# Order of DVE and ACT at seven places of a decoder layer, and products with v ahead of the scores

## The chip, the cores and the metric

The kernel runs on one core of one Trainium2 chip. The metric is device time in microseconds (us). A core has engines that run their own instruction queues in order and meet through semaphores: TensorE (PE, matrix products), VectorE (DVE), ScalarE (ACT), GpSimd (POOL) and SyncE (SP, which here issues transfers). Matrix products accumulate in PSUM; everything else lives in SBUF.

## The reference

One decoder layer on x of 1024 positions by 1024 features, in float32, with a pre-norm on each sub-layer. The mixer has two branches that are merged by gates; a gated MLP with a causal convolution of width 3 follows.

```
h = rmsnorm(x)
q, k, v, su, sv, g_a, g_b = split(h @ w_in)
y_att = sliding_window_attention(q, k, v)      # window 128, 8 query and 2 key heads of 64, ALiBi, sinks
y_sgu = gelu(su) * (tril(w_s) @ rmsnorm(gelu(sv)) + b_s)   # in chunks of 128 positions, 8 groups
x = x + (sigmoid(g_a) * (y_att @ w_oa) + sigmoid(g_b) * (y_sgu @ w_ob)) @ w_out
z = conv(rmsnorm(x) @ w_up)                    # per channel, over positions
gate, val = split(z)
x = x + (silu(gate) * val) @ w_down
```

The hidden width of the MLP is 2816, so w_up has 5632 columns (22 pairs of a gate block and a value block).

## The kernel before

**Precision.** Every float32 operand of a large product is split in a high part, rounded to PE's float32r by ACT (`copy_hi`, line 88), and a low part, the difference, taken by DVE or POOL. A product is three matmuls: high by high, high by low, low by high (`mm3`, lines 92 to 94). Lines 1120, 1700 and 2055 do the same in the later stages. So each operand passes ACT, then DVE or POOL, before PE reads it.

**Blocks.** From the gates on, products are done on two by two blocks with seven block products and sums of blocks (A11, B11, S1 to S4 and T1 to T4 are such blocks and sums). Sums are added on DVE while their parts sit in PSUM.

**Stages.** The span runs through: x, k and v, and the first q (to 45 us); the attention loop (`for n in range(20)`, to about 170); the spatial gating unit (`v_phase`, `v_end`, to 220); the gates; the branches (`B_UNITS`, y as the right operand, 355 to 445); the output product (`out_job`, 14 of them, 445 to 530); the MLP's up product with 22 pairs (`fast_pair`, to 960); the down product in seven products M1 to M7 (`mms`, to the end).

**What sets the order.** Every engine runs its instructions in the order in which the code issues them: the whole body is under a manual schedule. So the order of the lines is the order of the queues, and an instruction that waits holds all behind it on its engine.

**What the change touches.**

- k's evacuation: `k_hi` and `k_lo` empty a transposed k from PSUM (tile pk) into the high and low parts kT, one instruction for each of two row halves (line 397). `q_sq`, `q_ms`, `q_norm` square q's projection (tile pq), take its mean and the power on POOL (line 324, tile qss), and normalize it (line 330, tile qr). `v_evac` (line 407) scales v by rstd, a power on POOL (line 447), and line 140 spreads rstd over the partitions by matmuls (tile rb). `q_split` ends in the low parts qs (line 345).
- The attention loop is software-pipelined: step n issues scores of block n (`s_mm`, lines 484 and 487, tile sc), mask and maximum, exponentials of n-1, transposes and splits of n-2 (`p_trans`, `p_split`), products with v of n-4 (`pv_mm`, line 559, tile pv) and their result (`pv_out`, line 572, tile ya). A filler of projections stands between.
- The gating unit: `sgu_seed` (ACT, line 979) writes the bias into a PSUM tile pm, `sgu_mm` adds a product, `sgu_mul` (DVE, line 996, tile uT) multiplies the result into u and so empties the tile. `v_rsqrt`, `v_norm` and `v_split` prepare v for it.
- The branches: `y_split(br, n, eng)` makes the high (line 88) and low part (line 1294) of a block y; `hooks` are called between the products of a unit. Line 1360 is the low part of the weights (wjl, on POOL).
- The output: after product j = 0 and 1, ACT copies the result X to Y (line 1708), into which later products add. `O_WORK[j]` issues splits for coming products.
- `fast_pair`: the sums of a pair need x1, an ACT copy of one block product (line 1888). `prev.tap_v()` is the first tap of the convolution of the pair before (ACT, line 1741), `prev.last_sum()` the DVE sum and scale that it reads.
- The down product: `mms(g)` runs a group of k tiles, for each k over four rows d of output; `done(s)` adds a finished product to the result on DVE (`plus`, line 2092). The accumulators X are two PSUM tiles pdx with two rows d each.

Of the kernel before, what the change touches and what calls it, by code (L numbers as in the profile page):

```python
# [14 lines left out]
ALU = mybir.AluOpType  # L15
# [25 lines left out]
def body(ctx, tc, nc, a):  # L41
# [349 lines left out]

    def k_lo(h):
        cs = slice(512 * h, 512 * h + 512)
        pk = st.pop(("pk", h))
        for g in range(2):
            r = ROWS[g]
            nc.vector.scalar_tensor_tensor(kTl[r, g, cs], pk[r, :], kgq[r, 0:1], kTh[r, g, cs].bitcast(F),
                                           op0=ALU.mult, op1=ALU.subtract)
# [39 lines left out]
    q_proj(2)  # L438
    k_lo(0)
    q_norm(1)  # L440
    k_twice(0)
    q_trans(0)
# [3 lines left out]
    k_norm(1)  # L446
    nc.gpsimd.tensor_tensor(rstd, rstd, mh05, op=ALU.pow)
    q_split(0)
    q_norm(2)
    copy_hi(u_next[0], u_raw[0])  # L450
    nc.gpsimd.tensor_tensor(u_next[1], u_raw[0], u_next[0].bitcast(F), op=ALU.subtract)
    v_evac(0)
    v_evac(1)
    q_trans(1)
    k_trans(1)
    q_sq(3)
    q_split(1)
    q_ms(3)
    nc.vector.tensor_scalar(nsink, sink_b, -1.0, None, op0=ALU.mult)
    k_hi(1)  # L460
    rms_rows([PH("rb")], rstd, (0,))
    k_lo(1)
# [225 lines left out]
    man.__enter__()  # L688
    for n in range(20):
        if n < 16:  # L690
            s_mm(n)
            s_mask(n)
# [4 lines left out]
        if n < 16:  # L697
            s_max(n)
        if 0 <= n - 4 < 16:
            pv_mm(n - 4)  # L700
# [141 lines left out]
    def v_phase():  # L842
# [8 lines left out]
        for s in range(7):  # L851
            v_half(s, 1)
            if 4 <= s + 3 < 8:
                v_half(s + 3, 0)
            if s == 6:
                sgu_mm(0, 0)
            v_gelu(s)
            wb_copy(s)
            if s < 4:
                nc.scalar.activation(uT[:, s, :], uT[:, s, :], AF.Gelu_apprx_tanh)  # L860
            v_rsqrt(s)
            if s < 5:
                v_norm(s)
            if s in X_WORK:
                X_WORK[s]()
            if s > 0:
                v_split(s - 1)
            if s == 6:
                sgu_mul(0, 0)
            if s > 4:  # L870
                v_norm(s)
            if s in X_LATE:
                X_LATE[s]()
# [431 lines left out]
    def gates():  # L1305
# [6 lines left out]
        un["hooks"][1, 0] = lambda: (y_split("a", "T4"), y_split("a", "T1", nc.gpsimd))  # L1312
        un["hooks"][2, "x"] = lambda: (y_split("a", "T2", nc.gpsimd), y_hi("a", "B22"))
        un["hooks"][2, 0] = lambda: y_lo("a", "B22")
# [374 lines left out]
    def out_job(j):  # L1689
# [3 lines left out]
        def main(w):  # L1693
# [3 lines left out]
            for d in (0, 1):  # L1697
                for k in range(4):
                    for i, (p, q) in enumerate(((w[0], 0), (w[0], 1), (w[1], 0))):
                        nc.tensor.matmul(ob[o][e][:, d, :], p[:, 4 * d + k, :], m[:, q, k, :],  # L1700
                                         start=s in (0, 5) and k == 0 and i == 0, stop=k == 3 and i == 2,
                                         skip_group_check=True)
            O_WORK.get(j, lambda: None)()
            yield
            if j == 0:
                ob["Y"] = [PS("pY").rearrange("p (d c) -> p d c", d=2) for _ in range(2)]
            if s == 0:
                nc.scalar.copy(ob["Y"][e], ob["X"][e])
            else:
                {10: post10, 11: post11, 12: post12, 13: post13}.get(j, lambda: o_post(s, e))()  # L1710
# [159 lines left out]
    def fast_pair(n, prev, q, hooks, rms=None):  # L1870
# [6 lines left out]
        if rms:  # L1877
            x1 = temp("x1f", "wx")
        else:
            prev.last_sum()  # L1880
            prev.tap_v()
            x1, x7, q.u2 = temp("x1"), temp("x7"), temp("u2")
# [3 lines left out]
        if not nx:  # L1886
            hooks[2]()
        nc.scalar.copy(x1, q.g0)  # L1888
        if rms:
            rms()  # L1890
# [57 lines left out]
    def mlp():  # L1948
# [93 lines left out]
        def mms(g):  # L2042
# [8 lines left out]
            for k in range(k0, k1):  # L2051
                for d in range(4):
                    m = slice(128 * d, 128 * d + 128)
                    for j, (p, q) in enumerate(((ah, bh), (ah, bl), (al, bh))):
                        nc.tensor.matmul(o[d], p[:, k - k0, m], q[:, k - k0, :],  # L2055
                                         start=new and k == 0 and j == 0, stop=k == HK - 1 and j == 2,
                                         skip_group_check=True)

        def mms_last():

# [80 lines left out]
        for g in range(len(groups)):  # L2141
            if g < len(groups) - 2:
                mms(g)
# [111 lines left out]
```

## Time and profile before

| | us |
|---|---|
| median of 3 runs | 1163.71 (1163.32 to 1163.99) |
| profiled execution | 1162.16, span 1160.1 |
| PE busy | 1152.5 (99%), 5784 matmuls |
| DVE, ACT, POOL busy | 853.1 (74%), 589.9 (51%), 662.5 (57%) |
| DMA | 204.37 MB, 176 GB/s in the mean; granted clock of PE 0.999 |

Busy times are of the one profiled execution. In the rows of a timeline the first two numbers are the start from the span's beginning and the duration in us; then engine, line of the kernel, operation, output<-inputs by the program's names, sizes, and how many like instructions are merged (their duration is from the first start to the last end). The bracket is the idle time of the engine just before and what ended it. Matmuls overlap, so the distance of starts, not the duration, is what one costs. PE idles before its first matmul and after its last (the last results are written out from about 1156.4 on); between these the idle time is a few waits, each under 0.6 us.

### The profile page before, as it was taken

What the parts mean: (1) busy time and instruction counts of PE and PEld (TensorE: products, weight loads), DVE (VectorE), ACT (ScalarE), POOL (GpSimd) and SP (SyncE); (2) the same over time, 40 slices, a digit from 0 to 9 for tenths busy, and PEclk for the clock granted to TensorE, in tenths of its full rate; (3) what the DMA queues carried; (4) which work ended last, traced back from release to release, by engine and by line L of the source; (5) the groups of instructions that cost most, each with busy time, mean ns of one, the idle gap of its engine ahead of it and who ended that gap; (6) DMA issues with size and microseconds to landing.
All of it is one profiled execution on the core that took longest, in us unless ns stands there. A gap on an engine that the chain in (4) does not pass through costs nothing.

```text
span 1160.1 us, 15819 instructions
## 1 busy us (share of the span) xinstructions
PE 1152.5 (99%) x5784; PEld 978.5 (84%) x5784; DVE 853.1 (74%) x985; ACT 589.9 (51%) x896; POOL 662.5 (57%) x462
## 2 busy tenths in 40 slices
PE   9999999999999999999999999999999999999998
PEld 9999999888888888888888888888888888888887
DVE  7777746734537889877888878797878887766674
ACT  6665568643436546676544444444444454425231
POOL 1668684597883844798877676767676730000000
PEclk9999999999999999999999999999999999999999
DMA  9442575266646766634655554545464368965571
GB/s 365 150 146 57 133 220 191 92 187 194 191 118 227 244 218 236 190 128 129 163 173 138 162 129 143 160 140 139 134 171 132 97 216 301 356 219 199 175 228 55
DMA packets 86429, 204.37 MB, mean 176 GB/s; under 512 B 9616, under 2 KB 17296, under 8 KB 86160
## 3 DMA queue, kind: packets, MB, share of 16 engines
q1 hardware_dynamic: 77280, 174.93, 43.7%
q0 software_dynamic: 8544, 19.93, 10.5%
q10 hardware_dynamic: 528, 8.52, 2.1%
q8 instruction: 45, 0.74, 0.3%
q14 instruction: 32, 0.26, 0.1%
HBM read 162.70 MB, written 57.41 MB: 190 GB/s over the span
## 4 chain that ended last, share of the span: by engine, by line
PE 85%; DVE 5%; POOL 3%; DMA 2%; ACT 2%; issue 1%; SPq 0%; DVEq 0%; ACTq 0%; POOLq 0%
PE pz L1120 51%; PE pdx L2055 10%; PE pd L2055 8%; PE pY L1700 2%; PE pX L1700 1%; PE pu L94 1%; PE pu L92 1%; PE pu L93 1%; PE pv L559 1%; DMA xr<-xw 1%; PE pq L92 1%; PE pq L94 1%; PE pq L93 1%; POOL sq L1547 1%; DMA xt<-xt 1%
## 5 line engine op out<-in xcount | busy, mean ns | idle before, releaser
L1120 PE MATMUL pz<-T,qh 128*128 128x512 f32 x464 | 143.0, 389 | 0.0
L1120 PE MATMUL pz<-B,ph 128*128 128x512 f32 x352 | 108.9, 390 | 0.5 <-ACT x L1888 0.4
L1120 PEld LDWEIGHTS pz<-T,qh 128*128 128x128 f32 x464 | 87.0, 188 | 18.4 <-ACT u L937 0.3
L1072 POOL TENSOR_TENSOR pl<-lp,ph 128x1024 fp32r<-128x1024 f32 x30 | 73.7, 2456 | 36.3 <-ACT ph L88 36.3
L1120 PE MATMUL pz<-T,ql 128*128 128x512 f32 x232 | 90.2, 389 | 0.0
L1138 DVE TENSOR_TENSOR pz<-pz,rstd_b 128x1024 f32<-128x1024 f32 x60 | 74.0, 1232 | 6.1 <-ACT rstd_b L143 4.1
L1120 PEld LDWEIGHTS pz<-B,ph 128*128 128x128 f32 x352 | 65.8, 188 | 14.7 <-ACT x L1888 1.3
L1072 POOL TENSOR_TENSOR ql<-lq,qh 128x1024 fp32r<-128x1024 f32 (+1 forms) x31 | 76.5, 2490 | 0.1
L1120 PE MATMUL pz<-T,s3h 128*128 128x512 f32 x232 | 71.4, 389 | 0.0
L1120 PE MATMUL pz<-y,wjh 128*128 128x512 f32 x224 | 69.6, 391 | 0.4 <-POOL y L1294 0.4
L1120 PE MATMUL pz<-B,pl 128*128 128x512 f32 x176 | 68.5, 389 | 0.0
L88 ACT ACTIVATE qh<-lq 128x1024 fp32r<-128x1024 f32 (+1 forms) x31 | 31.5, 1021 | 67.7 <-POOL pl L1072 50.3
L1072 POOL TENSOR_TENSOR s3l<-lq,s3h 128x512 fp32r<-128x512 f32 x20 | 26.0, 1300 | 68.2 <-ACT s3h L88 68.2
L2055 PE MATMUL pdx<-bh,ah 128*128 128x512 f32 x164 | 63.9, 390 | 0.1
L2055 PE MATMUL pdx<-bl,ah 128*128 128x512 f32 x164 | 63.8, 389 | 0.0
L2055 PE MATMUL pdx<-bh,al 128*128 128x512 f32 x164 | 63.8, 389 | 0.0
L1360 POOL TENSOR_TENSOR wjl<-wj,wjh 128x512 fp32r<-128x512 f32 (+1 forms) x32 | 41.9, 1329 | 33.7 <-ACT wjh L88 27.0
L1120 PE MATMUL pz<-T,AX 128*128 128x512 f32 x252 | 60.5, 389 | 0.0
L1120 PE MATMUL pz<-B,AX 128*128 128x512 f32 x252 | 60.5, 389 | 0.0
L1746 DVE SCALAR_TENSOR_TENSOR tg<-pz,cp,tg 128x1023 f32<-128x1023 f32 (+1 forms) x44 | 56.2, 1278 | 0.8
L1746 DVE SCALAR_TENSOR_TENSOR tv<-pz,cp,tv 128x1023 f32<-128x1023 f32 (+1 forms) x44 | 56.2, 1278 | 0.8
L1120 PEld LDWEIGHTS pz<-T,AX 128*128 128x128 f32 x252 | 47.3, 188 | 9.8
(392 smaller groups left out, 3574.7 us busy)
## 6 DMA issues: line engine op xcount, KB each, us to landing
lp<-wup SPq DMA_DIRECT2D x22, 512.0 KB, 3.8
lq<-wup SPq DMA_DIRECT2D x22, 512.0 KB, 4.0
ra<-wdown SPq DMA_DIRECT2D x44, 256.0 KB, 4.6
b<-T SPq DMA_DIRECT2D x44, 256.0 KB, 3.4
lq<-wup POOLq DMA_DIRECT2D x42, 256.0 KB, 5.4
B<-tv SPq DMA_DIRECT2D x33, 256.0 KB, 2.4
T<-tt SPq DMA_DIRECT2D x33, 256.0 KB, 2.2
b<-B SPq DMA_DIRECT2D x33, 256.0 KB, 3.0
```

The costliest lines, as they stand in the source:

```text
L88: return nc.scalar.activation(dst, src, AF.Copy, scale=scale)
L92: nc.tensor.matmul(out, wh, mh, start=first, stop=False, **kw)
L93: nc.tensor.matmul(out, wh, ml, start=False, stop=False, **kw)
L94: nc.tensor.matmul(out, wl, mh, start=False, stop=last, **kw)
L559: nc.tensor.matmul(o, vhl[:, kb, g, :], w[:, 2 * g:2 * g + 2, :], start=i == 0 and g == 0, stop=i == len(ops) - 1, skip_group_check=True)
L1072: nc.gpsimd.tensor_tensor(l, r, h.bitcast(F), op=ALU.subtract)
L1120: nc.tensor.matmul(o, p[:, k, :], m, start=not more and k == 0 and j == 0, stop=k == nk - 1 and j == 2, skip_group_check=True)
L1138: nc.vector.tensor_tensor(z, z, rstd_b, op=ALU.mult)
L1360: nc.gpsimd.tensor_tensor(l[:, k], r[:, k], h[:, k].bitcast(F), op=ALU.subtract)
L1700: nc.tensor.matmul(ob[o][e][:, d, :], p[:, 4 * d + k, :], m[:, q, k, :], start=s in (0, 5) and k == 0 and i == 0, stop=k == 3 and i == 2, ...
L1746: nc.vector.scalar_tensor_tensor(t[:, j:], p[:, 0:1024 - j], cw[:, ci, 2 - j:3 - j], t[:, j:], op0=ALU.mult, op1=ALU.add)
L2055: nc.tensor.matmul(o[d], p[:, k - k0, m], q[:, k - k0, :], start=new and k == 0 and j == 0, stop=k == HK - 1 and j == 2, skip_group_check= ...
```

## The change

The places, numbered in the order of the program, as the prediction names them:

1. k's evacuation: the two low parts of the first half of k are split, with `q_norm(1)` between them. The power of rstd goes ahead of that of q 2 on POOL. `v_evac(0)` goes ahead of `q_norm(2)`, `v_evac(1)` behind `q_split(1)`, and on ACT the copy of the spread rstd ahead of `k_hi(1)`.
2. Attention: in the steps 4 to 11 the products with v are issued ahead of the scores (on PE alone).
3. Gating unit: `sgu_mul(0, 0)` goes ahead of `v_rsqrt(6)` and `v_split(5)`.
4. Branches: the low part of y block T2 of branch a is taken by DVE instead of POOL.
5. Output: the copy after product 1 is issued ahead of that product's `O_WORK`.
6. and 7. Up product: in pairs 2 and 3 the copy x1 goes ahead of `prev.tap_v`.
8. Down product: the last two groups of M5 are run together, all k of a row d before the next d (`mms_two`).

```diff
--- before.py
+++ after.py
@@ -389,10 +389,10 @@
         for g in range(2):
             copy_hi(kTh[ROWS[g], g, cs], pk[ROWS[g], :], scale=kgq[ROWS[g], 0:1])
 
-    def k_lo(h):
+    def k_lo(h, gs=(0, 1)):
         cs = slice(512 * h, 512 * h + 512)
-        pk = st.pop(("pk", h))
-        for g in range(2):
+        pk = st[("pk", h)]
+        for g in gs:
             r = ROWS[g]
             nc.vector.scalar_tensor_tensor(kTl[r, g, cs], pk[r, :], kgq[r, 0:1], kTh[r, g, cs].bitcast(F),
                                            op0=ALU.mult, op1=ALU.subtract)
@@ -436,29 +436,30 @@
     k_trans(0)
     k_hi(0)
     q_proj(2)
-    k_lo(0)
+    k_lo(0, (0,))
     q_norm(1)
+    k_lo(0, (1,))
+    nc.gpsimd.tensor_tensor(rstd, rstd, mh05, op=ALU.pow)
     k_twice(0)
     q_trans(0)
     q_proj(3)
     q_sq(2)
     q_ms(2)
     k_norm(1)
-    nc.gpsimd.tensor_tensor(rstd, rstd, mh05, op=ALU.pow)
     q_split(0)
-    q_norm(2)
     copy_hi(u_next[0], u_raw[0])
     nc.gpsimd.tensor_tensor(u_next[1], u_raw[0], u_next[0].bitcast(F), op=ALU.subtract)
     v_evac(0)
-    v_evac(1)
+    q_norm(2)
     q_trans(1)
     k_trans(1)
     q_sq(3)
     q_split(1)
+    v_evac(1)
     q_ms(3)
     nc.vector.tensor_scalar(nsink, sink_b, -1.0, None, op0=ALU.mult)
+    rms_rows([PH("rb")], rstd, (0,))
     k_hi(1)
-    rms_rows([PH("rb")], rstd, (0,))
     k_lo(1)
     v_split()
     k_twice(1)
@@ -687,6 +688,8 @@
     man = tc.manual_schedule()
     man.__enter__()
     for n in range(20):
+        if 4 <= n < 12:
+            pv_mm(n - 4)
         if n < 16:
             s_mm(n)
             s_mask(n)
@@ -696,7 +699,7 @@
             s_exp(n - 1)
         if n < 16:
             s_max(n)
-        if 0 <= n - 4 < 16:
+        if 12 <= n:
             pv_mm(n - 4)
         q_new = filler(n, 0)
         if 0 <= n - 2 < 16:
@@ -858,6 +861,8 @@
             wb_copy(s)
             if s < 4:
                 nc.scalar.activation(uT[:, s, :], uT[:, s, :], AF.Gelu_apprx_tanh)
+            if s == 6:
+                sgu_mul(0, 0)
             v_rsqrt(s)
             if s < 5:
                 v_norm(s)
@@ -865,8 +870,6 @@
                 X_WORK[s]()
             if s > 0:
                 v_split(s - 1)
-            if s == 6:
-                sgu_mul(0, 0)
             if s > 4:
                 v_norm(s)
             if s in X_LATE:
@@ -1310,7 +1313,7 @@
         un["hooks"][0, 0] = lambda: y_split("a", "B21", nc.gpsimd)
         un["hooks"][1, "x"] = lambda: y_split("a", "T3")
         un["hooks"][1, 0] = lambda: (y_split("a", "T4"), y_split("a", "T1", nc.gpsimd))
-        un["hooks"][2, "x"] = lambda: (y_split("a", "T2", nc.gpsimd), y_hi("a", "B22"))
+        un["hooks"][2, "x"] = lambda: (y_split("a", "T2"), y_hi("a", "B22"))
         un["hooks"][2, 0] = lambda: y_lo("a", "B22")
         nc.vector.tensor_scalar(ng2, g2, -1.0, None, op0=ALU.mult)
         un["hooks"][3, 1] = lambda: (m_split("B11", 0), m_sum("T1", 0))
@@ -1700,13 +1703,15 @@
                         nc.tensor.matmul(ob[o][e][:, d, :], p[:, 4 * d + k, :], m[:, q, k, :],
                                          start=s in (0, 5) and k == 0 and i == 0, stop=k == 3 and i == 2,
                                          skip_group_check=True)
+            if j == 1:
+                nc.scalar.copy(ob["Y"][1], ob["X"][1])
             O_WORK.get(j, lambda: None)()
             yield
             if j == 0:
                 ob["Y"] = [PS("pY").rearrange("p (d c) -> p d c", d=2) for _ in range(2)]
-            if s == 0:
-                nc.scalar.copy(ob["Y"][e], ob["X"][e])
-            else:
+            if j == 0:
+                nc.scalar.copy(ob["Y"][0], ob["X"][0])
+            elif j > 1:
                 {10: post10, 11: post11, 12: post12, 13: post13}.get(j, lambda: o_post(s, e))()
             O_AFTER.get(j, lambda: None)()
             if j == 13:
@@ -1878,7 +1883,8 @@
             x1 = temp("x1f", "wx")
         else:
             prev.last_sum()
-            prev.tap_v()
+            if n not in (2, 3):
+                prev.tap_v()
             x1, x7, q.u2 = temp("x1"), temp("x7"), temp("u2")
         q.prod(q.g0, "A11", "B11")
         if rms:
@@ -1886,6 +1892,8 @@
         if not nx:
             hooks[2]()
         nc.scalar.copy(x1, q.g0)
+        if n in (2, 3):
+            prev.tap_v()
         if rms:
             rms()
             lefts[n].split_r(n)
@@ -2056,6 +2064,16 @@
                                          start=new and k == 0 and j == 0, stop=k == HK - 1 and j == 2,
                                          skip_group_check=True)
 
+        def mms_two(g):
+
+            two = [(k, k - groups[i][1], ops_[i]) for i in (g - 1, g) for k in range(*groups[i][1:])]
+            for d in range(4):
+                m = slice(128 * d, 128 * d + 128)
+                for k, i, (ah, al, bh, bl) in two:
+                    for j, (p, q) in enumerate(((ah, bh), (ah, bl), (al, bh))):
+                        nc.tensor.matmul(X[d], p[:, i, m], q[:, i, :], start=False,
+                                         stop=k == HK - 1 and j == 2, skip_group_check=True)
+
         def mms_last():
 
             two = [(k, k - groups[g][1], ops_[g]) for g in (len(groups) - 2, len(groups) - 1)
@@ -2139,7 +2157,9 @@
         q = prev
         n_load = 4
         for g in range(len(groups)):
-            if g < len(groups) - 2:
+            if g == 6 * len(GR) - 1:
+                mms_two(g)
+            elif g < len(groups) - 2 and g != 6 * len(GR) - 2:
                 mms(g)
             s, k0, k1 = groups[g]
             while n_load < min(g + 6, len(groups)):
```

What DVE does at k's evacuation, before (pq and qr are of q, pk and kT of k, vt of v):

```order
L397 SCALAR_TENSOR_TENSOR kT_107<-pk_515,kgq,kT_107 64x512 x2
L330 TENSOR_TENSOR qr_549<-pq_477,qss_507 128x256
L322 TENSOR_REDUCE qss_583<-qsq_581 128x4
L323 TENSOR_SCALAR qss_583<-qss_583,eps_x 128x4
L376 TENSOR_TENSOR kr<-pkv_126,krs 128x512
L345 TENSOR_TENSOR qs_589<-pqt_553,qs_589 64x256 x2
L330 TENSOR_TENSOR qr_594<-pq_522,qss_583 128x256
L407 TENSOR_TENSOR vt<-pkv_125,rstd 128x512
L407 TENSOR_TENSOR vt<-pkv_126,rstd 128x512
L345 TENSOR_TENSOR qs_610<-pqt_600,qs_610 64x256 x2
```

and now:

```order
L397 SCALAR_TENSOR_TENSOR kT_107<-pk_515,kgq,kT_107 64x512
L330 TENSOR_TENSOR qr_548<-pq_477,qss_507 128x256
L397 SCALAR_TENSOR_TENSOR kT_107<-pk_515,kgq,kT_107 64x512
L322 TENSOR_REDUCE qss_584<-qsq_582 128x4
L323 TENSOR_SCALAR qss_584<-qss_584,eps_x 128x4
L376 TENSOR_TENSOR kr<-pkv_126,krs 128x512
L345 TENSOR_TENSOR qs_589<-pqt_554,qs_589 64x256 x2
L407 TENSOR_TENSOR vt<-pkv_125,rstd 128x512
L330 TENSOR_TENSOR qr_597<-pq_522,qss_584 128x256
L345 TENSOR_TENSOR qs_609<-pqt_599,qs_609 64x256 x2
L407 TENSOR_TENSOR vt<-pkv_126,rstd 128x512
```

`q_norm(1)` (qr_548) now stands between the two kT, the first vt ahead of the next qr, and the low parts of the next q ahead of the second vt.

What ACT does at the start of pair 2, before (tv and tg are taps of the pair before, x_731 is x1, pz are PSUM tiles):

```order
L1132 COPY u_716_5646<-pz_5443 128x512
L88 ACTIVATE AX_5638<-lr_5710 128x1024
L1741 ACTIVATE tv_5768<-pz_5443,cp 128x1024
L1888 COPY x_731_5770<-pz_5764 128x512
L1741 ACTIVATE tg_5786<-pz_5442,cp 128x1024
```

and now:

```order
L1135 COPY u_716_5646<-pz_5443 128x512
L88 ACTIVATE AX_5638<-lr_5710 128x1024
L1894 COPY x_730_5768<-pz_5764 128x512
L1746 ACTIVATE tv_5784<-pz_5443,cp 128x1024
L1746 ACTIVATE tg_5786<-pz_5442,cp 128x1024
```

The copy x1 (line 1894 now) and the tap tv have changed places; in pair 3 the same.

What DVE does in the branch unit with the y block T2 (y_539) and the block after it (y_503), before:

```order
L1400 TENSOR_TENSOR pz_4145<-u_534_4149,pz_4145 128x512
L1407 SCALAR_TENSOR_TENSOR m_4233<-th_4104,pz_4145 128x1024
L1407 SCALAR_TENSOR_TENSOR m_4235<-th_4106,pz_4146 128x1024
L663 TENSOR_TENSOR x_550_4240<-x_550_4240,pz_4237 128x512
L1294 TENSOR_TENSOR y_503_3990<-ya_3157,y_503_3990 128x1024
L1394 TENSOR_TENSOR pz_4238<-x_549_4239,pz_4238 128x512
```

and now:

```order
L1403 TENSOR_TENSOR pz_4145<-u_534_4149,pz_4145 128x512
L1410 SCALAR_TENSOR_TENSOR m_4233<-th_4104,pz_4145 128x1024
L1410 SCALAR_TENSOR_TENSOR m_4235<-th_4106,pz_4146 128x1024
L1297 TENSOR_TENSOR y_539_4191<-ta,y_539_4191 128x1024
L664 TENSOR_TENSOR x_550_4240<-x_550_4240,pz_4237 128x512
L1297 TENSOR_TENSOR y_503_3990<-ya_3157,y_503_3990 128x1024
L1397 TENSOR_TENSOR pz_4238<-x_549_4239,pz_4238 128x512
```

The low part y_539 has come in from POOL, between the products m of the unit before and the subtraction x; on POOL the weights' low parts (wjl) follow one another there.

## The prediction

> **What bounds the kernel now.** I read the busy shares first, then what PE waited for, then the timelines of the engines around each wait. PE is busy for 1152.5 of the 1160.1 us, and the change neither adds nor removes a matmul; all it can win is PE's idle time. The waits of PE, by cause (engine, tile and line that waited <- releaser: total us, times, longest):
>
> ```profile
> PE pq L92 <- DVE kT L397: 0.6, 1, 0.6
> PE pm L92 <- ACT pm L979: 0.5, 1, 0.5
> PE pz L1120 <- ACT x L1888: 0.4, 1, 0.4
> PE pz L1120 <- POOL y L1294: 0.4, 1, 0.4
> PE pY L1700 <- ACT pY L1708: 0.3, 1, 0.3
> ```
>
> Each happens once, and each lies at one of the places that the diff touches; a sixth, 0.20 us, is in the row at 43.25 below. Elsewhere PE issues without a break, so the sum goes place by place. A wait costs a little more than its idle time. Two pairs of rows (start us, duration us) show it:
>
> ```profile
> 566.94 0.39 PE L1120 MATMUL pz<-B,pl 128*128 128x512 f32 x1
> 569.66 0.39 PE L1120 MATMUL pz<-T,s3l 128*128 128x512 f32 x1
> 570.48 0.50 PE L1120 MATMUL pz<-B,ph 128*128 128x512 f32 x1 [0.43 <-ACT x L1888]
> 589.43 0.39 PE L1120 MATMUL pz<-T,s3l 128*128 128x512 f32 x1
> 589.85 0.73 PE L1120 MATMUL pz<-B,ph 128*128 128x512 f32 x2
> 568.75 1.21 ACT L1741 ACTIVATE tv<-pz,cp 128x1024 f32<-128x1024 f32 x1 [1.74 <-DVE pz L1138]
> 569.86 0.57 ACT L1888 COPY x<-pz 128x512 f32<-128x512 f32 x1
> ```
>
> Unhindered, such a matmul starts 0.23 us after the one before: two take 0.62 and one 0.39 in the rows at 396.44 and 569.66. From 569.66 to 570.48 are 0.82 us, so 0.59 lost; the first matmul after the wait lasts 0.50 instead of 0.39, so 0.11 more: 0.70 in all. At 589.43 it is 0.42 to the next start, 0.19 lost, and again about 0.11: 0.30.
>
> **The two products of the gated MLP (places 6 and 7).** ACT copies x1, which PE waits for, after prev.tap_v, and that waits for DVE until 568.75. The product that x1 is copied from ends at 566.94 + 0.39 = 567.33; put first, the copy runs in ACT's idle 1.74 us, from 567.4 to 568.0. tap_v then finds ACT free when DVE releases it, so nothing behind it is later. In the second pair ACT has the same pattern. No other wait of PE stands near either place. I take the whole of both, **1.00 us**; bounds 0.70 (if only the first goes) and 1.00.
>
> **k's evacuation (place 1).**
>
> ```profile
> 37.30 0.36 PE L92 MATMUL pq<-wq,x 128*128 128x256 f32 x1 [0.58 <-DVE kT L397]
> 40.95 1.16 PE L140 MATMUL rb<-ident,rstd 128*128 128x128 f32 x8
> 43.25 0.57 PE L140 MATMUL rb<-ident,rstd 128*128 128x128 f32 x3 [0.20 <-DVE qs L345]
> 35.64 1.51 DVE L397 SCALAR_TENSOR_TENSOR kT<-pk,kgq,kT 64x512 fp32r<-64x512 f32 x2 [0.24 <-issue]
> 39.69 0.42 DVE L330 TENSOR_TENSOR qr<-pq,qss 128x256 f32<-128x256 f32 x1
> 42.25 0.86 DVE L345 TENSOR_TENSOR qs<-pqt,qs 64x256 fp32r<-64x256 f32 x2
> 38.28 1.01 POOL L324 TENSOR_TENSOR qss<-qss,mh 128x4 f32<-128x4 f32 x1 [0.57 <-DVE qss L323]
> 39.26 1.64 POOL L447 TENSOR_TENSOR rstd<-rstd,mh 128x8 f32<-128x8 f32 x1
> ```
>
> The two kT instructions end at 37.15 and PE starts 0.15 later. With q's normalization between them, PE's buffer needs the first kT (0.76) and one qr (0.42): 35.64 + 0.76 + 0.42 + 0.15 = 36.97, so 0.33 earlier. Most of this does not last. POOL now raises rstd (1.64 us) ahead of q's next qss: from 38.28 - 0.57 = 37.71 to 39.36, then qss to 40.37; DVE normalizes q to 40.80, and the rb matmuls at 40.95, whose buffer that frees, start at about 40.94. What lasts is the second rb: the low parts of q that held it until 43.11 (42.25 + 0.86) now stand ahead of v's second evacuation and end near 41.9, so its 0.20 us of idle, 0.37 from start to start by the same reckoning as above, and 0.07 of restart go. Sum: 0.01 + 0.44 = **0.45 us**; bounds 0.3 and 0.8 (if the first 0.33 lasted too). The low part of k's second half is later by some 0.2 us; the first score that reads it comes after more than 4 us of other matmuls.
>
> **Scores and products with v (place 2).**
>
> ```profile
> 98.14 0.40 PE L559 MATMUL pv<-eh,vhl 128*128 128x256 f32 x2
> 99.09 0.28 PE L92 MATMUL pq<-wq,x 128*128 128x256 f32 x1
> 101.48 0.85 DVE L572 TENSOR_TENSOR ya<-pv,o 64x256 f32<-64x256 f32 x2
> 102.49 0.48 PE L484 MATMUL sc<-kT,qs 128*128 128x256 f32 x2
> ```
>
> The eight products with v of a step take 99.09 - 98.14 = 0.95 us (the first of the eight steps has four, 0.47). Putting them ahead of the scores moves work within PE's queue, without a gap to close: 0 expected. What it adds is a tighter wait: the products of step 9 need the buffer that ya empties at 101.48 + 0.85 = 102.33 and would now start at 102.49, 0.16 later, with 0.15 us seen from DVE's end to PE's start at 37.15 above. The scores come 0.95 later to the mask and the additions on DVE, which have other work until about then; step 6, whose ya follows such a mask, ends up as tight as step 9, and the other steps have more room. I take **0**; bounds: a gain of 0.1, a loss of 0.45 (what k won, if ya keeps its own time).
>
> **The seed of the sixth product of the gating unit (place 3).**
>
> ```profile
> 204.22 0.68 DVE L814 TENSOR_TENSOR vsl<-vg,vsh 128x512 fp32r<-128x512 f32 x1
> 204.82 1.38 DVE L996 TENSOR_TENSOR uT<-pm,uT 64x512 f32<-64x512 f32 x2
> 206.30 1.03 ACT L979 ACTIVATE pm<-rb 128x1024 f32<-128x1024 f32 x1 [1.56 <-DVE uT L996]
> 207.38 0.39 PE L92 MATMUL pm<-wgh,vsh 128*128 128x256 f32 x1 [0.51 <-ACT pm L979]
> ```
>
> ACT seeds PE's buffer once DVE has emptied it (uT). Ahead of v_split and the small v_rsqrt, uT starts at 204.22 instead of 204.82: 0.60 earlier, and ACT, which idles 1.56 us there, follows. PE's start becomes 206.78. That leaves 0.51 - 0.60 below nothing by the idle time alone; with the 0.16 us by which a start-to-start loss exceeds it, some 0.08 us and the restart stay. I take **0.59 us**; bounds 0.5 and 0.79. The displaced split feeds products of the second half only, which come after 214 us.
>
> **The low part of y (place 4).**
>
> ```profile
> 392.73 2.39 POOL L1294 TENSOR_TENSOR y<-ta,y 128x1024 fp32r<-128x1024 f32 x1
> 395.09 2.27 POOL L1360 TENSOR_TENSOR wjl<-wj,wjh 128x512 fp32r<-128x512 f32 x1
> 393.95 2.25 DVE L1294 TENSOR_TENSOR y<-ya,y 128x1024 fp32r<-128x1024 f32 x1
> 395.18 0.50 PE L1120 MATMUL pz<-y,wjh 128*128 128x512 f32 x1 [0.35 <-POOL y L1294]
> 396.44 0.62 PE L1120 MATMUL pz<-y,wjh 128*128 128x512 f32 x2
> ```
>
> PE waits at 395.18 for POOL. DVE does the same subtraction in 1.2 us (2.25 less the 1.17 from 393.95 to POOL's end at 395.12: the two rows show DVE held until POOL is done, then POOL's wjl held until DVE is). Two inputs in SBUF on both engines exclude each other here. So on DVE y would be ready near 394.2 and the 0.62 us of this stall would go; but POOL's wjl then starts at 394.2, as soon as DVE lets go, holds the next low part (the 393.95 row, needed by PE's second matmul of the 396.44 row, at 396.67) until 395.3, and that ends near 396.4: PE starts at 396.55 instead of 396.67, and pays the restart again. I take **0.05 us**; bounds 0 and 0.62. The Trainium skill, "SBUF — State Buffer", section "Who interferes with whom", has this as a rule: a DVE instruction with two SBUF inputs and a GpSimd one that reads SBUF block each other fully, and issue order decides who waits. It speaks against moving this work from POOL to DVE; by it the place gives nothing, without it 0.62, and these rows side with it.
>
> **The copy of pY (place 5).**
>
> ```profile
> 458.49 2.20 ACT L88 ACTIVATE mT<-mraw 128x1024 fp32r<-128x1024 f32 x2 [2.85 <-DVE mraw L667]
> 461.72 1.37 POOL L1571 TENSOR_TENSOR wjl<-wj,wjh 128x512 fp32r<-128x512 f32 x1 [6.68 <-ACT wjh L88]
> 463.17 0.46 PE L1700 MATMUL pY<-mB,wjl 128*128 128x512 f32 x1
> ```
>
> The copy moves into ACT's 2.85 us of idle time and PE's 0.33 us wait for it goes. But the third matmul, at 463.17, needs wjl, which POOL ends at 463.09: the wait moves two matmuls on. wjl follows a cast on ACT that the copy did not delay. **0 us**; bounds -0.1 and 0.6.
>
> **The last product groups (place 8 of the diff, mms_two).**
>
> ```profile
> 1124.66 1.29 DVE L2092 SCALAR_TENSOR_TENSOR res<-pdx,res 128x512 f32<-128x512 f32 x2 [1.57 <-PE pdx L2055]
> 1126.02 1.29 DVE L2092 SCALAR_TENSOR_TENSOR res<-pdx,res 128x512 f32<-128x512 f32 x2
> 1126.10 0.47 PE L2055 MATMUL pdx<-bh,ah 128*128 128x512 f32 x1
> 1127.57 0.39 PE L2055 MATMUL pdx<-bh,ah 128*128 128x512 f32 x1
> ```
>
> PE idled 0.11 us before 1126.10, by the reckoning above a loss of about 0.35, waiting for the first two additions (the second ends at 1125.95). With the rows d done one after the other these run earlier, but d 2 and 3 are still finished where they were, near 1126.0, and their additions end at 1127.31; PE wants them at 1127.57 less the gain, 1127.2, and gets them at 1127.46. I take **0.05**; bounds 0 and 0.35.
>
> **Sum.** 1.00 + 0.45 + 0 + 0.59 + 0.05 + 0 + 0.05 = 2.14 us. The profiled execution, 1162.16 us with 1160.1 of span, becomes 1160.0. It lies 1.55 below the median of 1163.71, so the median becomes **1161.6**.
>
> **The rivals.** *All stalls go*: the waits do not move on at places 4, 5 and 8, giving 0.62 + 0.60 + 0.35 instead of 0.10, so 3.6 us: 1160.1. For it: ordering could let DVE take the low part of y before wjl; against it: the rows of POOL. Chance 0.25. *The gains upstream are eaten*: ya keeps its time at step 9, k's 0.45 is lost, and half of the 0.59 at the gating unit: 1162.4, chance 0.12. *The attention loop closes on DVE* and ends slower: the scores of eight steps come 0.95 later, and if mask, softmax and product of a step then no longer fit ahead of the next, each step pays. Seven steps at 0.95 and one at 0.47 are 7.1 us; less 2.1 gives 1168.7. It decides once ya ends later than 102.34; the idle time of DVE in the loop speaks against it. Chance 0.06. *The change does nothing*, since PE's waits reappear at the next matmul everywhere: 1163.5, chance 0.04.
>
> **How the numbers follow.** The forecast has 0.53. A measurement here tells 0.2%, 2.33 us, from no change, so 1161.38 is the edge, 0.2 below the forecast. Its own range is 1160.9 to 1162.3 (bounds of places 1, 3 and 4), of which I give 0.40 to the faster side. Faster: 0.53 x 0.40 + 0.25 x 0.97 = 0.45. Slower: 0.07 with the loop and small unseen losses. Same: 0.48. The range, 1159.9 to 1163.0, takes in the forecast, all stalls gone and eaten gains, and leaves out the slow loop and the nothing.
>
> **What would show it.** In the profile of the changed kernel: the waits on kT, the seed pm and x L1888 gone or under 0.15 us; new waits of PE on a DVE low part of y near 394, on wjl near 462, and on DVE near 1125; no wait of PE between 70 and 130 us. Wrong would be a PE wait on ya, or the three handed-on waits missing.

## The result, and the profile after

The change takes 1160.19 us in the median (1158.26 to 1163.43, 21 runs), the kernel before in the same sessions 1163.46 (1161.85 to 1164.77, 21 runs): ratio 0.9973, 95% interval 0.9967 to 0.9980. That is 3.3 us less (2.3 to 3.8 by the interval). The forecast was 1161.6, 2.1 us less; the time lies in the range of 1159.9 to 1163.0, 0.3 us above its lower end. It is beyond the edge of 0.2%, an outcome to which the prediction gave 0.45; its likeliest outcome, a difference too small to tell, had 0.48.

The profiled execution of the change took 1160.19 us, its median, with a span of 1158.5. That of the kernel before, 1162.16, was near the low end of its runs; a second one, below, took 1164.29. So single profiles are compared here place by place, between the same matmuls, not by their spans.

What PE waited for after the change, in the view of waits:

```profile
PE warm L255 <- POOL rstd_b L120: 1.1, 1, 1.1
PE pY L1703 <- POOL wjl L1574: 0.4, 1, 0.4
PE rb L140 <- DVE qr L330: 0.3, 1, 0.3
PE pz L1123 <- DVE y L1297: 0.3, 1, 0.3
```

The waits on kT, on x1 and on the seed pm are gone. The first row is of the start of the program and is in the kernel before too. In the other three, wjl in place of the copy of pY and DVE's low part of y in place of POOL's are waits that the prediction handed on; DVE's qr ahead of the spread of rstd belongs to the start that it put at 40.94. The third handed-on wait, near 1125, has too little idle time for this view. PE's rows where these waits end, and those of pair 2:

```profile
36.94 0.36 PE L92 MATMUL pq<-wq,x 128*128 128x256 f32 x1
...
41.00 0.38 PE L140 MATMUL rb<-ident,rstd 128*128 128x128 f32 x1 [0.34 <-DVE qr L330]
...
42.94 0.60 PE L140 MATMUL rb<-ident,rstd 128*128 128x128 f32 x4
...
395.97 0.50 PE L1123 MATMUL pz<-y,wjh 128*128 128x512 f32 x1 [0.26 <-DVE y L1297]
...
462.54 0.50 PE L1703 MATMUL pY<-mB,wjl 128*128 128x512 f32 x1 [0.41 <-POOL wjl L1574]
...
569.14 0.39 PE L1123 MATMUL pz<-T,s3l 128*128 128x512 f32 x1
569.37 0.62 PE L1123 MATMUL pz<-B,ph 128*128 128x512 f32 x2
...
1125.39 0.39 PE L2063 MATMUL pdx<-bh,al 128*128 128x512 f32 x1
1125.80 0.50 PE L2063 MATMUL pdx<-bh,ah 128*128 128x512 f32 x1
```

The prediction had put the matmul at 36.94 at 36.97 and that at 41.00 at 40.94. In pair 2 it is 0.23 us from 569.14 to the next start; before, it was 0.82. From 1125.39 to 1125.80 it is 0.41 instead of 0.23, so a part of that stall is left, six matmuls later. Near 396 DVE and POOL exclude each other as forecast:

```profile
393.33 3.73 POOL L1363 TENSOR_TENSOR wjl<-wj,wjh 128x512 fp32r<-128x512 f32 x2 [1.04 <-ACT wjh L88]
```

```profile
392.46 1.22 DVE L1297 TENSOR_TENSOR y<-ta,y 128x1024 fp32r<-128x1024 f32 x1
...
394.19 1.72 DVE L1297 TENSOR_TENSOR y<-ya,y 128x1024 fp32r<-128x1024 f32 x1
```

The first low part takes 1.22 us, the second, which meets wjl, 1.72 and ends at 395.91, where PE starts.

**What was not forecast** is in the attention loop. It has no waits to lose, and yet its steps got shorter. From the first matmul behind the transposes of q in step 5 to the next transposes PE runs the same 40 matmuls of 256 columns, before in 80.29 - 75.50 = 4.79 us:

```profile
75.50 0.48 PE L484 MATMUL sc<-kT,qs 128*128 128x256 f32 x2
...
80.06 0.28 PE L93 MATMUL pq<-wq,x 128*128 128x256 f32 x1
80.17 0.28 PE L94 MATMUL pq<-wq,x 128*128 128x256 f32 x1
80.29 0.60 PE L529 MATMUL pt<-ident,c 128*128 128x128 f32 x4
```

and after the change in 79.87 - 75.20 = 4.67 us:

```profile
75.20 0.48 PE L560 MATMUL pv<-eh,vhl 128*128 128x256 f32 x2
...
79.53 0.28 PE L92 MATMUL pq<-wq,x 128*128 128x256 f32 x1
79.64 0.28 PE L93 MATMUL pq<-wq,x 128*128 128x256 f32 x1
79.75 0.28 PE L94 MATMUL pq<-wq,x 128*128 128x256 f32 x1
79.87 0.60 PE L530 MATMUL pt<-ident,c 128*128 128x128 f32 x4
```

Two neighbouring starts lie 0.12 us apart before and 0.11 after, without idle time in either. In full resolution there are two values, 113 to 114 and 117 to 118 ns (called 113 and 118 ns below), and long streams keep one of them. Between 170 and 201 us, in v's projection, it is the other way round. The matmuls that run in the 12 us from 172 to 184, before (the columns are stretch, its length, then busy us and number for PE, weight loads, DVE, ACT and POOL, then PE's granted clock, and share and GB/s of the DMA):

```profile
172.00:184.00 12.00, 12.00 (x108) 12.00 (x107) 2.99 (x6) 9.66 (x16) 6.01 (x5) 1.00 0.91 343
```

and after:

```profile
172.00:184.00 12.00, 12.00 (x104) 12.00 (x103) 3.00 (x6) 10.09 (x16) 6.44 (x6) 1.00 0.89 330
```

PE's clock is granted in full in both (1.00). Over v's projection the longer step costs 301 x 4.5 ns, about 1.3 us. In the profile of the change this gave back all that the places 1 and 2 had won: against the first profile of the kernel before, matmul by matmul, PE was 0.96 us ahead at the end of the last products with v and 0.31 behind at the first product pm. But PE then came late enough for the seed pm to be ready, and without a wait there it was 0.44 ahead behind it.

### The profile page after: what moved, and what is told of

Its sections match the earlier page's. It is cut to its first block, busy times and chain, and to the rows that moved or that the text cites. A ratio compares the mean times of both kernels' runs of the same rounds, so it can differ in the third digit from the quotient of the medians.

```text
span 1158.5 us, 15802 instructions
## 1 busy us (share of the span) xinstructions
PE 1152.6 (99%) x5784; PEld 979.9 (85%) x5784; DVE 856.2 (74%) x986; ACT 589.5 (51%) x896; POOL 661.0 (57%) x461
## 4 chain that ended last, share of the span: by engine, by line
PE 98%; DVE 1%; ACT 0%; issue 0%; POOL 0%; DVEq 0%; POOLq 0%; ACTq 0%
PE pz L1123 55%; PE pdx L2063 9%; PE pd L2063 8%; PE pX L1703 4%; PE pY L1703 3%; PE pvs L92 1%; PE pvs L94 1%; PE pvs L93 1%; PE pu L94 1%; PE pu L92 1%; PE pu L93 1%; PE pv L560 1%; PE pq L92 1%; PE pq L93 1%; PE pq L94 1%; PE pdx L2085 1%
## 5 line engine op out<-in xcount | busy, mean ns | idle before, releaser
L2063 PE MATMUL pdx<-bh,ah 128*128 128x512 f32 x152 | 59.2, 390 | 0.0
L2063 PE MATMUL pdx<-bh,al 128*128 128x512 f32 x152 | 59.1, 389 | 0.0
L2063 PE MATMUL pdx<-bl,ah 128*128 128x512 f32 x152 | 59.1, 389 | 0.0
L1135 ACT COPY u<-pz 128x512 f32<-128x512 f32 x28 | 16.4, 587 | 80.6 <-DVE pz L1134 80.6
```

Of the source, the lines that this page charges most:

```text
L1135: nc.scalar.copy(self.u2, self.v1)
L2063: nc.tensor.matmul(o[d], p[:, k - k0, m], q[:, k - k0, :], start=new and k == 0 and j == 0, stop=k == HK - 1 and j == 2, skip_group_check= ...
```

## The experiments

All times are against the kernel before, run on the same chip in the same session; three sessions of four kernels. Theory A: the queues' order and the waits alone decide, as predicted. Theory B: PE's two steps of 113 and 118 ns decide a part; B1 says that a wait sets the longer one, B2 that it is chance.

**Place 2 alone (e1).**

```diff
     for n in range(20):
+        if 4 <= n < 12:
+            pv_mm(n - 4)
         if n < 16:
             s_mm(n)
...
-        if 0 <= n - 4 < 16:
+        if 12 <= n:
             pv_mm(n - 4)
```

> The kernel before with place 2 alone: products with v ahead of the scores in steps 4 to 11. Theory A (the order of PE's queue and its waits alone decide): no wait is removed, so 0.0 us, within 0.2 of the kernel before, and the attention loop from 70 to 130 us takes as long as before. Theory B (matmuls of 256 columns run in one of two cadences, about 113 and 118 ns from start to start, as the two traces show, and the order of a step decides which one its stream falls into): the loop gets about 0.7 us shorter, as in the profile of the change (from 0.42 to 1.04 us earlier between 80 and 129 us), most intervals there turning from 118 to 113 ns. Under B the long stream of v's projection (168 to 201 us, some 285 matmuls) may fall into either cadence, worth 1.3 us.

1162.49 us against 1163.61, ratio 0.9989 (0.9980 to 0.9998). The loop got shorter as B says: over 430 matmuls, from the first transposes of the steps with place 2 on, 57.75 us against 58.36. Theory A is wrong here. v's projection ran at 118 ns, and no wait for pm is in its list of waits, though place 3 is not in this kernel.

**The change without place 2 (e2).** The diff is that of e1 taken back.

> The change without place 2, all other places as in the change. Theory A: the full gain of the change, since place 2 is worth nothing: 2.1 us by the prediction's sum. Theory B: the loop keeps 118 ns over most of the steps 4 to 11 and the gain is smaller than the change's by about 0.7 us; PE reaches the last products with v 0.7 us later than in the change, finds POOL's low part cl ready, and the stream of v's projection behind it runs at 113 ns.

1160.33 us, ratio 0.9973 (0.9962 to 0.9984): the change's own ratio. The loop took 58.36 us, as before. So within the loop place 2 is worth 0.6 to 0.8 us, in each of eight profiles with it and in none of six without. In the total e1 was just clear of no change, while taking place 2 out of the change cost nothing that could be seen: how much of it reaches the total is open. The expectation that v's projection would run at 113 ns was wrong: 105 matmuls ran in its 12 us, nearly as in the change, and PE waited a little for cl.

**The last products with v behind the filler (e3).**

```diff
-        if 12 <= n:
+        if 12 <= n < 19:
             pv_mm(n - 4)
         q_new = filler(n, 0)
+        if n == 19:
+            pv_mm(n - 4)
```

> The change, with the products with v of the last attention step issued behind that step's filler of v's projection instead of ahead of it. In the profile of the change PE waits 0.08 us there for POOL's cl (167.22 to 167.41 us) and the 301 matmuls behind it run at 118 ns, where the kernel before, without that wait, ran 285 of them at 113 ns. Theory B1 (that small wait sets the slow cadence): the stream runs at 113 ns, 1.3 us are won against the change's profile, and the time is lower than the change's by about 1 us. Theory B2 (the cadence of the stream is a matter of chance in each execution): no systematic gain; the time is the change's within 0.5 us, and the cadence of the stream is one or the other.

1166.89 us, ratio 1.0023 (1.0013 to 1.0033): slower. The stream did run at 113 ns, but PE now waited long for DVE's vg, once in v's projection, which was called ahead of the products, and once at the first product of the gates, pz (that the PSUM tiles are dealt out in the order of the calls, and so in another turn, would explain it, but was not tested):

```profile
PE pvs L92 <- DVE vg L815: 2.7, 1, 2.7
PE pz L1125 <- DVE vg L815: 2.2, 1, 2.2
PE warm L255 <- POOL rstd_b L120: 1.1, 1, 1.1
PE pm L92 <- ACT pm L984: 0.9, 1, 0.9
```

So it cannot tell what the shorter step is worth in the total; e5 below takes away the wait for cl without changing PE's order.

**The change without places 4, 5 and 8 (e4).**

```diff
-        un["hooks"][2, "x"] = lambda: (y_split("a", "T2"), y_hi("a", "B22"))
+        un["hooks"][2, "x"] = lambda: (y_split("a", "T2", nc.gpsimd), y_hi("a", "B22"))
...
-            if j == 1:
-                nc.scalar.copy(ob["Y"][1], ob["X"][1])
...
-            if g == 6 * len(GR) - 1:
-                mms_two(g)
```

> The change without the places 4, 5 and 8 (low part of y on DVE, copy of pY earlier, last groups of M5 together). The prediction: these give 0.10 us together because each wait moves on to the next instruction, so the time is the change's within 0.3 us, and the stalls near 394, 462 and 1125 us are there as in the kernel before, 0.62, 0.60 and 0.35 us from start to start. The rival (all stalls go): 1.5 us slower than the change.

1161.60 us, ratio 0.9980 (0.9970 to 0.9990). The interval overlaps the change's, so the total does not tell. In the trace the three stalls of the kernel before are back at their old size, and the stretches around them are longer than in the change by 0.05 to 0.11 (by where the stretch is cut), 0.00 and 0.06 us.

**The last selects ahead of the weights z0 (e5).**

```diff
-WHEN = {"u1": 0, "q0": 1, "q1": 2, "u2": 5, "u3": 9, "v0": 13, "v1": 14, "z0": 16, "z1": 17}
+WHEN = {"u1": 0, "q0": 1, "q1": 2, "u2": 5, "u3": 9, "v0": 13, "v1": 14, "z0": 17, "z1": 17}
```

> The change, with the weights z0 split one step later, so that on POOL the last selects of the attention stand ahead of the low part of z0 (2.43 us) instead of behind it. PE's order is the change's. It takes away PE's wait for cl near 167.2 us by having cl ready some 2.4 us sooner. Theory B1 (that wait puts the stream of v's projection behind it into the slow cadence): over 270 of its 256-column matmuls between 170 and 200 us run at 113 ns, that stage is 1.3 us shorter than in the change, and the time is about 1 us below the change's (ratio to the kernel before near 0.996). Theory B2 (chance in each execution): the slow cadence may stay, time as the change's. Theory A (only waits count): 0.1 us.

1162.31 us, ratio 0.9994 (0.9985 to 1.0003). No wait for cl, and v's projection ran at 113 ns:

```profile
172.00:184.00 12.00, 12.00 (x109) 12.00 (x108) 3.12 (x6) 8.49 (x13) 6.00 (x5) 1.00 0.98 349
```

but the kernel is not faster. Its ratio lies above the change's, 0.9973 (0.9967 to 0.9980), without overlap, so this edit lost most of the change's gain. In its profile the time came back as a wait for the seed pm, 0.9 us, with place 3 in the kernel:

```profile
PE pm L92 <- ACT pm L982: 0.9, 1, 0.9
```

Here PE's step in v's projection did not set the end of that stage; DVE's and ACT's work up to the seed did, which ended 1.3 us later than in the change (the edit moves some of that work, too). This profile is of the fastest of the 11 runs, 1160.94 us, so most of the loss in the median is in no trace.

**The last select done twice (e6).**

```diff
+        if n == 15:
+            last_sel[0] = nc.gpsimd.affine_select(out=cl, in_=cl.bitcast(F), pattern=[[0, 4], [1, 128]],
+                                                  compare_op=ALU.is_ge, fill=0.0, base=0,
+                                                  channel_multiplier=-1)
         st[("p", n)].append((eh, el, b - 1))
```

> The kernel before, with the last select of the attention (cl) done twice on POOL, 0.6 us more there; the second does not change the data. PE's order is that of the kernel before. Its slack at cl was 0.43 us, so PE now waits about 0.2 us near 168.3. Theory B1: the stream of v's projection behind it falls from 113 to 118 ns, 1.3 us, so with the wait about 1.5 us slower than the kernel before (ratio near 1.0013). Theory B2: no systematic turn to 118 ns. Theory A: 0.2 to 0.3 us slower, no measurable difference.

1163.81 us, ratio 1.0009 (1.0000 to 1.0018). PE waited 1.2 us for cl, more than expected, and v's projection ran at 118 ns, as B1 says; no wait for pm was left.

**Place 2 in the steps 12 to 15 too (e7).**

```diff
-        if 4 <= n < 12:
+        if 4 <= n < 16:
             pv_mm(n - 4)
...
-        if 12 <= n:
+        if 16 <= n:
             pv_mm(n - 4)
```

on top of e5.

> The kernel of the run with the selects first, and the products with v ahead of the scores in the steps 12 to 15 too. Theory B: in these steps too part of the matmuls turn from 118 to 113 ns, as in the steps 4 to 11, 0.1 us for each step that has both: 0.3 to 0.4 us less between 130 and 160 us than in the kernels before and after, where this stretch has 58 fast and 82 slow intervals. Theory A: 0, or a loss where the products with v now wait.

1162.73 us, ratio 0.9999 (0.9991 to 1.0008). No faster than e5. The step did turn, but less than expected: in step 12, 23 of its 35 intervals were short instead of 1, and up to its transposes of q it took 4.66 instead of 4.76 us; in the steps 13 to 15, 6 of 45 instead of 14. What step 12 won was lost to a new wait: a product with v waited 0.3 us for ya in step 13, the wait that the prediction feared at step 9. v's projection and pm waited 0.9 us each:

```profile
PE pm L92 <- ACT pm L982: 0.9, 1, 0.9
PE pvs L92 <- DVE vg L813: 0.9, 1, 0.9
...
PE pv L560 <- DVE ya L573: 0.3, 1, 0.3
```

**wjh ahead of the casts of T2 (e8),** on top of e7.

```diff
-        1: lambda: (m_split("T2", 0), m_split("T2", 1), m_lo("B22", 0), out_load("22")),
+        1: lambda: out_load("22"),
...
     O_AFTER = {
+        1: lambda: (m_split("T2", 0), m_split("T2", 1), m_lo("B22", 0)),
```

> The kernel of the run before this one, and in the output product the cast wjh ahead of the casts and low parts of T2 on ACT and DVE, so that POOL takes wjl some 2 us sooner. In the change the wait of place 5 had moved on to wjl (0.41 us idle, 0.69 from start to start near 462 us). The prediction's reasoning for place 5: with wjl sooner both waits are gone and the 0.69 us are won, with no new wait, since T2 is first read near 467 us. The rival: the DVE's and POOL's low parts block each other and the wait moves on once more, to mB or T2.

1164.58 us, ratio 1.0016 (1.0005 to 1.0026). The wait for wjl at the fourth product is gone, and there is one at the sixth, larger than the 0.41 it replaced; the output products together took 0.6 us longer than in e7.

```profile
PE pX L1704 <- POOL wjl L1574: 0.6, 1, 0.6
```

In this stage POOL and DVE take turns: two of wjl's pairs of low parts took 4.1 us each, against 2.55 for the pair ahead of them (3.6 and 4.5 in e7), and DVE's pair of low parts mT took 4.25 instead of the 2.36 of e7:

```profile
454.30 2.55 POOL L1574 TENSOR_TENSOR wjl<-wj,wjh 128x512 fp32r<-128x512 f32 x2 [1.55 <-ACT wjh L88]
460.74 4.07 POOL L1574 TENSOR_TENSOR wjl<-wj,wjh 128x512 fp32r<-128x512 f32 x2 [3.89 <-ACT wjh L88]
465.17 4.09 POOL L1574 TENSOR_TENSOR wjl<-ow,wjh 128x512 fp32r<-128x512 f32 x2 [0.37 <-ACT wjh L88]
```

**The kernel before, once more (e9),** unchanged.

> The kernel before, unchanged, as a second execution to look into and as a measure of what no change looks like. Ratio to itself 1.000 within its interval. If the cadence of v's projection is set by the wait for cl, its stream runs at 113 ns here as in the first profile, since PE has 0.43 us of slack there; if it is chance, it may run at 118 ns. The start of the program (9 to 33 us) has shown both cadences in the same code in the ten profiles so far (8 fast, 2 slow), so it may be either.

1163.67 against 1163.53 us, ratio 0.9996 (0.9987 to 1.0004): what no change looks like. Its profile differs from the first by 2.2 us of span, most of it in two places. PE left the start of the program 1.5 us later, there at 118 ns, of which 0.9 was left behind k's evacuation, and it waited for cl, which the first profile did not:

```profile
169.82 0.50 PE L559 MATMUL pv<-cl,vhl 128*128 128x256 f32 x2 [0.52 <-POOL cl L547]
```

v's projection behind it ran at 118 ns. So this wait and the longer step occur in the kernel before as well; the first profile was one without them.

**The change without place 3 (e10).**

```diff
-            if s == 6:
-                sgu_mul(0, 0)
             v_rsqrt(s)
...
                 v_split(s - 1)
+            if s == 6:
+                sgu_mul(0, 0)
```

> The change without place 3 (sgu_mul ahead of v_split). The prediction: 0.59 us slower than the change, PE waiting again about 0.5 us for the seed pm near 206 us. The theory from the runs so far: PE waits for cl, its stream of v's projection runs at 118 ns and comes 1.3 us later to pm, so that the seed is ready with or without place 3 (as in the run with place 2 alone, which has no wait for pm): no wait for pm, time as the change's within 0.3 us.

1160.62 us, ratio 0.9976 (0.9966 to 0.9985), 0.4 us above the change and within the interval. In its profile there was a wait for cl, and v's projection ran at 113 ns all the same, and PE waited 1.2 us for pm:

```profile
PE pm L92 <- ACT pm L982: 1.2, 1, 1.2
...
PE pv L560 <- POOL cl L548: 0.5, 1, 0.5
```

B1 is wrong as a rule: the wait does not set the step. And the expectation of no wait for pm was wrong for this execution.

**Places 4, 5 and 8 alone (e11).** The diff is that of e4, the other way, on the kernel before.

> The kernel before with the places 4, 5 and 8 alone. The prediction: 0.10 us in all, no measurable difference, with waits of PE for the low part of y on DVE near 396, for wjl near 463 and for DVE near 1126 us in place of the three of before, each within 0.15 us of them. The rival (all stalls go): 1.5 us faster.

1163.54 against 1163.53 us, ratio 0.9994 (0.9985 to 1.0002): no difference, as predicted, though the interval would just allow the rival's 1.5 us (0.9987). The traces decide: the three waits have new owners and nearly the old size; two of them in PE's rows:

```profile
396.83 0.50 PE L1120 MATMUL pz<-y,wjh 128*128 128x512 f32 x1 [0.26 <-DVE y L1294]
...
463.38 0.50 PE L1700 MATMUL pY<-mB,wjl 128*128 128x512 f32 x1 [0.42 <-POOL wjl L1571]
```

**Places 6 and 7 alone (e12).**

```diff
-            prev.tap_v()
+            if n not in (2, 3):
+                prev.tap_v()
...
         nc.scalar.copy(x1, q.g0)
+        if n in (2, 3):
+            prev.tap_v()
```

> The kernel before with the places 6 and 7 alone (the copy x1 ahead of prev.tap_v in pairs 2 and 3). The prediction: 1.00 us faster, ratio 0.9991, both waits of PE for x1 gone and no other in their place; all other waits as in the kernel before.

1162.11 against 1163.53 us, ratio 0.9985 (0.9976 to 0.9993). No wait for x1 in its list, and none in its place. The expected 0.9991 lies in the interval. The same 280 matmuls take 63.47 us here and 64.5 to 65.1 in the five profiles without the two places: 1.0 to 1.6 us, because the wait for x1 itself was 0.4 to 1.0 us in them.

None of these kernels is faster than the change.

## Why the prediction was right, and where it was not

It was right in its range, and in part by luck: 1160.19 is below the forecast's own 1160.9 to 1162.3 and lies in the range because this was widened for *all stalls go*, a rival that did not occur. (The bounds of the places 1, 3 and 4, from which those figures are said to come, add up to 1160.5 to 1161.9; and the rival with the gains eaten comes to 1162.3, not 1162.4.) Its sum was 2.14 us, and the measurement 3.3 (2.3 to 3.8); by its own steps, with what lies between the same two matmuls in the profiles with and without a place:

| place | predicted | in the traces |
|---|---|---|
| 1, k | 0.45 | 0.44 in the mean (60 matmuls across k's evacuation: 7.6 to 8.0 us in eight profiles with it, 8.0 to 8.4 in six without) |
| 2, attention | 0 | 0.6 to 0.8 in the loop |
| 3, seed pm | 0.59 | seed 0.65 sooner on DVE; gain of PE not shown |
| 4, low part of y | 0.05 | 0.1 |
| 5, copy of pY | 0 | 0.0 |
| 6 and 7, x1 | 1.00 | 1.0 to 1.6 |
| 8, last groups | 0.05 | 0.06 |

**Right.** The two pairs carried the largest part, and e12 shows it alone. The stall near 37 us went and came back ahead of the spread of rstd at 41.00; what lasted was the second spread, which runs on at 42.94 without a wait: the 15 matmuls around it take 1.72 us in each profile with place 1 and 2.16 in each without. No run has place 1 alone, so its worth is read from the traces. Of the three handed-on waits two came where they were put, with the owners that were named, and of the third a distance of 0.41 us is left. So the rival "all stalls go" did not occur: the change came out near its 1160.1 for other reasons.

**Wrong in mechanism: place 2.** The premise "all it can win is PE's idle time" and with it "Putting them ahead of the scores moves work within PE's queue, without a gap to close: 0 expected" failed. PE without idle time is not PE at one rate. Of the intervals between neighbouring matmuls of 256 columns in e1's stretch of the loop, nearly all were long before (301 of 302), and over half were short after (170 of 302). The bounds of this step, a gain of 0.1 and a loss of 0.45, missed it.

**Only conditional: place 3.** The 0.59 was read from one execution, in which PE waited 0.51 us for the seed. The wait depends on how early PE comes: it was 0.5 to 1.2 us in each of the eight profiles in which v's projection ran at 113 ns and absent in the six with 118 ns. With place 3 the wait was 0.9 in e5, without it 1.2 in e10; these differ in more than place 3, so its worth stays open. What the rows show is that the mechanism works on DVE. The T that stands ahead, before (its uT started at 204.82, 1.79 us behind this start):

```profile
203.03 1.22 DVE L825 TENSOR_TENSOR T<-xa,T 128x1024 fp32r<-128x1024 f32 x1
```

and after, 1.14 us, so 0.65 sooner where 0.60 was forecast:

```profile
202.57 1.22 DVE L828 TENSOR_TENSOR T<-xa,T 128x1024 fp32r<-128x1024 f32 x1
203.71 1.38 DVE L999 TENSOR_TENSOR uT<-pm,uT 64x512 f32<-64x512 f32 x2
```

In the profiles at 118 ns the seed was ready 0.67 to 0.69 us before PE started the matmul ahead of the one that needs it with place 3 (the change, e2, e4), and 0.02 to 0.07 before it without (e1, e6, e9): there PE gained nothing by it. In the profiles at 113 ns it is the seed, and not PE, that sets this point.

**The rival "the gains upstream are eaten"** was put at the wrong place, ya at step 9, but the effect exists: what the change's profile had won up to the last products with v was lost again in v's projection, and the change without place 2 has the same time as with it. The loop's 0.7 was in no case of the prediction; whether it made up for such losses in the total is not shown. The rival of a loop bound by DVE did not occur; no product with v waited for ya in the change, but in e7 one did.

**Mis-sized:** 6 and 7 by up to 0.6 us, for the same reason as place 3: a wait was taken from one profile as if it were fixed.

**Overlooked:** 0.3 us lie outside the span, where no wait of PE is seen. The device time exceeds the span by 2.0 us in the mean of the kernel before and of e1, e4, e9 and e12, by 1.9 in e6, and by 1.7 to 1.8 in the change and in every kernel here with the places 4, 5 and 8 (e2, e3, e5, e7, e8, e10, e11). So one of these places, or all together, gives 0.3 us that the prediction did not have; which, and why, no run shows.

The sum of these gains without place 3, 0.4 + 0.7 + 0.1 + 1.2 + 0.1 + 0.3, is 2.8 us, which lies in the measured interval. It counts the loop's 0.7 in full; what is missing to 3.3 is not assigned.

## What to carry to other kernels

Follow each removed wait to the next instruction that needs a late producer: three of the stalls here moved by two to six matmuls, and in one of them, as again in e8, the reason was a pair of engines, DVE and POOL, that hold each other up when both read from SBUF. A stall read from one profile is one draw; where PE's arrival there depends on anything upstream, the gain is a range. And a stretch in which an engine never idles can still change its rate with the order of its instructions: compare the starts of like instructions, not only the gaps.

## What the runs showed of the hardware that was not expected

Matmuls of 256 columns with a 128 by 128 float32r weight load each ran in these traces at 113 to 114 ns or at 117 to 118 ns from start to start, at a granted clock of 1.00, and kept the value over up to 300 in a row. Nearly all turns in the 14 traces lie within a few matmuls of a change of product or of a short wait. The same code shows both: at the start of the program 9 profiles had the short and 5 the long step; in v's projection 8 and 6. There all five profiles in which PE came to cl without a wait ran at 113 ns over most of it; of the nine with a wait, some of them under 0.15 us, three did. A wait so seems to open the long step without setting it; the cause was not found. In the attention loop, by contrast, the short step came with the products with v ahead of the scores, in all 14 profiles. 512-column matmuls showed no such pair of values over long streams (227 ns).
